# RWKV-7 recurrence of a hybrid decoder layer: work units of one head pair and 512 tokens, against blocks of two head pairs and 256 tokens

## The chip, the cores and the metric

The kernel runs on 1 core of one Trainium2 chip, in one launch. The metric is device time of one execution in microseconds (us). The core has TensorE (PE in the profile, with its weight loads shown as PEld), VectorE (DVE), ScalarE (ACT), GpSimd (POOL), and SyncE (SP, which here only issues DMAs). Every engine runs its own instruction stream in order and waits on semaphores where an operand comes from another.

## The reference, cut to what matters

One layer: RMSNorm, one input projection (1024 to 512 + 1792 columns), a pooling mixer on 512 columns, RWKV-7 time mixing with 8 heads of 64 on the rest, an output projection, then a squared-ReLU MLP (1024 to 4096 to 1024). A prompt of 1024 tokens and 8 single decode tokens go through it.

```python
def step(S, inp):
    r_t, w_t, k_t, v_t, aa_t, bb_t = inp          # aa = -kk, bb = kk * a
    sa = jnp.einsum('bhvk,bhk->bhv', S, aa_t)
    S = S * w_t[:, :, None, :] + sa[..., None] * bb_t[:, :, None, :] + v_t[..., None] * k_t[:, :, None, :]
    return S, jnp.einsum('bhvk,bhk->bhv', S, r_t)
S_final, y = lax.scan(step, S0, xs)               # over the tokens
y = ((y - mu) * lax.rsqrt(var + GN_EPS)).reshape(B, T, RWKV_W) * ln_x_g + ln_x_b
y = (y + bonus.reshape(B, T, RWKV_W)) * g
mix = jnp.concatenate([pool_out, rwkv_out], axis=-1) @ w_out
x = x + mix;  x = x + jnp.square(jax.nn.relu(rmsnorm(x) @ w_up)) @ w_down
```

## The kernel before

The scan over 1024 tokens is done in chunks of 64. Two heads of 64 fill the 128 partitions and are called a head pair; there are four, `hp` 0 to 3. A **unit** is one head pair and one half (512 tokens, 8 chunks); there are eight, numbered 0 to 7, four of half 0 first. For each unit run, in this order:

- `rkv` (R in the order string): r, k and v are projected (`gemm`, L175) and token-shifted.
- `stage1` (S): decays and keys; then for each of the two 256-token parts of the unit the operands of the recurrence. `AR` holds scaled kk and r with masked score planes, `RB` and `AA` further score planes, all made out of the score matmuls (`sc`, L402) by DVE (L407, L409) and ACT. `BK` has three planes, and its transposition `BKT` is made once for each head, out of a 128x128 transposition of which half is kept (L419, L420). `vt` are the transposed values, which ACT writes into `SV` (L427). `AR` and `RB` come from a ring of four static segments.
- `inverse` (I): `AA` of all 8 chunks and both heads goes through DRAM (`blk`, L466) into `Dg` (L469); DVE solves the small blocks in `Xs` (L484 to L501), ACT writes them to `Es`, DMAs put them through DRAM into `TX` (L510 to L514), and PE and ACT build the 64x64 inverses `TT` (L522 to L549). There is one buffer each of `Xs`, `Es`, `Dg`, `tm`, `TX`, so inverses go one after the other; `TT` and the DRAM buffers are double.
- `chain` (C): 8 steps, one a chunk, each depending on the one before. On PE: `pq` (L575), `pa` with the inverse (L579), `pu` (L582), and two `py` matmuls (L576, L583) that only make the output. On ACT: `sg` (state times decay), `Q` (copy of pq), two copies of pa into `SV` (L592). On DVE: two updates that write the new state (L591). PE waits for ACT's Q, ACT for pa, PE for SV, DVE for pu, and PE for the new state. fp32 matmuls show as two passes each in the trace (x2).
- `post`: after each 256 tokens the group norm, bonus and gate of the `y` rows; the result `ys` goes to DRAM as `mix` (L596), on POOL's queue, which also issues all weight loads (`wr`, L157).

A scheduler fixes each engine's order ahead of time from priorities (chain first, `LEAD`; then inverse, `LEADI`) and from the string ORDER, in which P are parts of the pooling mixer, T and L the second half's tokens and low-rank gates, D the 8 decode tokens with their own states `dS`. Work of low priority, mostly the projections, stands between the steps on PE. When the last chain and the decode tokens are through, SP loads the `mix` rows of the second half (`mr`, L851) and `x` (L837), the output projection (`mx`) is finished, and the MLP (`up`, `dn`) follows.

Of the kernel before, what the change touches and what calls it, by code (L numbers as in the profile page):

```python
# [15 lines left out]
P = 128  # L16
# [23 lines left out]
ORDER = """R0 S0 R1 I0 S1 Q C0 R2 S2 I1 C1 R3 S3 I2 P00 P01 T I3 P02 L R4 C2 S4 C3 R5 S5 I4 R6 C4 S6 I5 R7 C5 S7 I6 C6 P10 I7 P11 P12 D"""  # L40
NBV = 3
# [43 lines left out]
def _build(ctx, nc, tc, I, O, dbg):  # L85
# [108 lines left out]
    def token_block(b):  # L194
# [6 lines left out]
        acc = big(f"acc{b}", "f" if b % 2 else "g")[:, :512].rearrange("p (k t) -> p k t", k=2)  # L201
# [133 lines left out]
    Sf = [zp.tile([P, 64], F32, name=f"Sf{hp}") for hp in range(4)]  # L335

    def stage1(U):
        hp, nm = U.hp, U.nm
        zw, za, _ = Zt[U.half]
        U.gam = rcp.tile([P, 8], F32, tag="gam", name=f"gam{nm}", bufs=4)  # L340
        U.AA = rcp.tile([P, 8 * 64 + 16], F32, tag="AA", name=f"AA{nm}", bufs=2)
        GP.memset(U.AA[:, 512:], 0.0)
        A3 = U.AA[:, 0:512].rearrange("p (c t) -> p c t", t=64)
# [40 lines left out]
        act(U.gam, Ep[:, :, 64])  # L384
        for i in range(2):
# [3 lines left out]
            seg = ring[0]  # L389
            ring[0] = (seg + 1) % NSEG  # L390
            AR, RB = U.AR[i], U.RB[i] = ARs[seg], RBs[seg]
            for h in range(2):
                rr = R[h]
                V.tensor_tensor(AR[rr, :, 0, h, :], r3(kk[rr, ls]), Ep[rr, cc, 0:64], op=ALU.mult)
                V.tensor_tensor(AR[rr, :, 1, h, :], r3(U.r[rr, ls]), Ep[rr, cc, 1:65], op=ALU.mult)
                V.tensor_tensor(BK[rr, :, 2 * h, :], r3(t[rr, ls]), Em[rr, cc, 1:65], op=ALU.mult)
            V.tensor_tensor(BK[:, :, 1, :], r3(U.k[:, ls]), Em[:, cc, 1:65], op=ALU.mult)

            scs = [ps_m.tile([P, 4, 128], F32, tag="m", name=f"sc{nm}_{h}") for h in range(2)]
            for c in range(4):  # L400
                for h in range(2):
                    PE.matmul(scs[h][:, c, :], BK[R[h], c, h:h + 2, :], AR[R[h], c, :, h, :], start=True, stop=True)  # L402
            for h in range(2):
                rr, ro = R[h], R[1 - h]
                psc = scs[h]
                act(A3[rr, 4 * i:4 * i + 4, :], psc[rr, :, 0:64])
                V.tensor_tensor(RB[rr, :, h, :], psc[rr, :, 64:128],  # L407
                                MS[rr, 64:128].unsqueeze(1).to_broadcast([64, 4, 64]), op=ALU.mult)
                V.tensor_tensor(AR[ro, :, :, h, :], psc[ro].rearrange("p c (a t) -> p c a t", t=64),  # L409
                                MS[ro].rearrange("p (a t) -> p a t", t=64).unsqueeze(1).to_broadcast([64, 4, 2, 64]),  # L410
                                op=ALU.mult)

# [8 lines left out]
            pv = ps_m.tile([P, 2, 128], F32, tag="m", name=f"vt{nm}")  # L421
            for c in range(2):
                PE.transpose(pv[:, c, :], U.v[:, 256 * i + 128 * c:256 * i + 128 * c + 128], ident)
            S2 = SV.rearrange("p (c e) h t -> p c e h t", e=2)
            for h in range(2):
                for e in range(2):
                    act(S2[R[1 - h], :, e, h, :], pv[R[e], :, 64 * h:64 * h + 64])  # L427

# [4 lines left out]
    BK = rcp.tile([P, 4, 3, 64], F32, name="BK")  # L433
    ring = [0]
    for t in (*ARs, *RBs, BK):
        GP.memset(t, 0.0)
# [20 lines left out]
    def inverse(U):  # L457
# [13 lines left out]
        with tc.high_priority(offset=LEADI):  # L471
# [598 lines left out]
```

## Time and profile before

| | |
|---|---|
| median of 3 runs | 1367.27 us (1367.04 to 1373.31) |
| the profiled execution | 1363.59 us, span 1361.8 us, mean granted clock 0.992 |
| busy over the span | PE 1298.1 us (95%), PEld 1144.8 (84%), DVE 823.2 (60%), ACT 592.4 (43%), POOL 156.3 (11%) |
| 0 to 577 us: projections, pooling mixer, recurrence, decode tokens | PE 525.14, DVE 435.38, ACT 424.71 |
| 577 us to the end: output projection of the second half, MLP | PE almost without a gap |

The page names the 20 costliest groups of instructions first; nearly all of them are of `gemm`. The recurrence is spread over some 300 small groups and is read from the timeline and from the tiles' answers instead. Matmul ends are modelled, so PE's busy time also contains time in which it was not at its peak.

### The profile page before, as it was taken

Reading aid. Unit: us, or ns where it says so; the run is one execution under the profiler, and the core shown is the slowest. Engines: PE = TensorE matmul, PEld = TensorE weight load, DVE = VectorE, ACT = ScalarE, POOL = GpSimd, SP = SyncE. Lnnn points to the kernel's source line nnn. Section 1 sums busy time; section 2 is a strip of 40 time slices with the busy share of each in tenths; the row PEclk is TensorE's granted clock in tenths of the full one; section 3 lists DMA queues with packets and bytes.
Section 4 is the critical chain, followed back from the end, with each engine's and each line's share of the span. In section 5 each row is a group of like instructions: output and inputs, shape, how many; then the busy total and the mean of one; then the engine's idle time right before and its main releaser. Section 6 shows DMA issues by size and latency. Waiting matters only on the chain.

```text
span 1361.8 us, 24570 instructions
## 1 busy us (share of the span) xinstructions
PE 1298.1 (95%) x9844; PEld 1144.8 (84%) x9844; DVE 823.2 (60%) x1816; ACT 592.4 (43%) x1466; POOL 156.3 (11%) x306
## 2 busy tenths in 40 slices
PE   5999998999999889999999999999999999999996
PEld 5987777888777777798999999999999999999986
DVE  8887687768778666749634435445344354453447
ACT  7668777866777767526211112112111121121122
POOL 3201001210101021120100000000000000000000
PEclk9999999999999999999999999999999999999998
DMA  6322223321322362531111111111111111111103
GB/s 196 106 58 58 70 47 94 109 70 42 79 55 51 75 198 95 197 101 47 53 49 47 47 47 47 47 47 47 48 46 49 48 46 48 45 48 50 47 5 125
DMA packets 75315, 94.82 MB, mean 70 GB/s; under 512 B 46168, under 2 KB 52440, under 8 KB 75192
## 3 DMA queue, kind: packets, MB, share of 16 engines
q0 software_dynamic: 20480, 66.04, 15.0%
q1 hardware_dynamic: 53392, 25.36, 7.2%
q10 hardware_dynamic: 1328, 1.85, 0.4%
q8 instruction: 77, 1.26, 0.4%
q14 instruction: 38, 0.31, 0.1%
HBM read 79.67 MB, written 13.78 MB: 69 GB/s over the span
## 4 chain that ended last, share of the span: by engine, by line
PE 75%; DVE 10%; ACT 9%; issue 2%; DMA 2%; POOL 1%; DVEq 0%; SPq 0%; POOLq 0%; ACTq 0%
PE dn L175 26%; PE up L175 26%; PE pj L175 7%; PE mx L175 5%; ACT SV L92 2%; PE pcs L582 1%; DVE tm L498 1%; PE pcs L579 1%; ACT Es L92 1%; ACT TT L92 1%; PE bkt L419 1%; PE pcs L575 1%; PE sc L402 1%; DVE wl L165 1%; PE py L583 1%
## 5 line engine op out<-in xcount | busy, mean ns | idle before, releaser
L92 ACT ACTIVATE wh<-wr 128x512 fp32r<-128x512 f32 x230 | 143.6, 626 | 353.2 <-PE dn L175 276.2
L175 PE MATMUL up<-h2h,wl 128*128 128x260 f32 (+1 forms) x768 | 245.5, 320 | 0.0
L175 PE MATMUL up<-h2h,wh 128*128 128x260 f32 (+1 forms) x768 | 245.0, 320 | 0.5 <-DVE u L912 0.5
L175 PE MATMUL up<-h2l,wh 128*128 128x260 f32 (+1 forms) x768 | 244.8, 319 | 0.0
L175 PE MATMUL dn<-uh,wl 128*128 128x512 f32 (+1 forms) x720 | 231.0, 321 | 0.0
L175 PE MATMUL dn<-ul,wh 128*128 128x512 f32 (+1 forms) x720 | 230.6, 320 | 0.0
L175 PE MATMUL dn<-uh,wh 128*128 128x512 f32 (+1 forms) x720 | 230.3, 320 | 0.0
L951 DVE TENSOR_TENSOR x<-dn,x 128x260 f32<-128x260 f32 (+1 forms) x192 | 99.0, 516 | 189.9 <-PE dn L175 189.9
L175 PE MATMUL pj<-xh,wh 128*128 128x256 f32 (+1 forms) x576 | 173.5, 301 | 14.3 <-ACT wh L92 13.9
L165 DVE TENSOR_TENSOR wl<-wr,wh 128x512 fp32r<-128x512 f32 x230 | 156.3, 684 | 45.1 <-ACT wh L92 38.2
L175 PE MATMUL pj<-xl,wh 128*128 128x256 f32 (+1 forms) x576 | 171.6, 298 | 0.0
L175 PE MATMUL pj<-xh,wl 128*128 128x256 f32 (+1 forms) x576 | 168.9, 293 | 0.0
L175 PEld LDWEIGHTS up<-h2l,wh 128*128 128x128 f32 x768 | 144.5, 188 | 12.2 <-DVE h2l L894 0.4
L175 PEld LDWEIGHTS up<-h2h,wh 128*128 128x128 f32 x768 | 144.1, 188 | 11.7 <-DVE u L912 0.9
L175 PEld LDWEIGHTS up<-h2h,wl 128*128 128x128 f32 x768 | 144.4, 188 | 11.1
L92 ACT ACTIVATE uh<-u 128x260 fp32r<-128x260 f32 (+1 forms) x96 | 47.2, 492 | 238.5 <-DVE u L913 238.5
L175 PEld LDWEIGHTS dn<-ul,wh 128*128 128x128 f32 x720 | 135.4, 188 | 10.9 <-issue 0.2
L175 PEld LDWEIGHTS dn<-uh,wh 128*128 128x128 f32 x720 | 135.7, 188 | 10.5
L175 PEld LDWEIGHTS dn<-uh,wl 128*128 128x128 f32 x720 | 135.4, 188 | 10.6 <-issue 0.2
L175 PEld LDWEIGHTS pj<-xh,wh 128*128 128x128 f32 x576 | 110.5, 192 | 18.8 <-ACT wh L92 14.2
L912 DVE SCALAR_TENSOR_TENSOR u<-up,rs 128x260 f32<-128x260 f32 (+1 forms) x96 | 49.5, 516 | 120.7 <-PE up L175 114.2
L175 PEld LDWEIGHTS pj<-xl,wh 128*128 128x128 f32 x576 | 110.5, 192 | 3.1 <-issue 1.9
(295 smaller groups left out, 2184.2 us busy)
## 6 DMA issues: line engine op xcount, KB each, us to landing
wr<-in_w_in POOLq DMA_DIRECT2D x72, 256.0 KB, 2.9
wr<-in_w_up POOLq DMA_DIRECT2D x64, 256.0 KB, 2.9
wr<-in_w_down POOLq DMA_DIRECT2D x64, 256.0 KB, 2.9
wr<-in_w_out POOLq DMA_DIRECT2D x26, 256.0 KB, 3.1
xr<-in_xT SPq DMA_DIRECT2D x16, 256.0 KB, 3.7
mr<-mix SPq DMA_DIRECT2D x8, 260.0 KB, 3.2
x<-in_xT SPq DMA_DIRECT2D x2, 1040.0 KB, 8.3
blk<-AA SPq DMA_DIRECT2D x16, 128.0 KB, 2.7
```

Source lines behind the costliest of these rows:

```text
L92: A.activation(out, in_, func, bias=bias, scale=scale, **k)
L165: V.tensor_tensor(l[:, :w], raw[:, :w], f32(h[:, :w]), op=ALU.subtract)
L175: PE.matmul(ps, lhs, rhs, start=i == 0, stop=i == n - 1)
L402: PE.matmul(scs[h][:, c, :], BK[R[h], c, h:h + 2, :], AR[R[h], c, :, h, :], start=True, stop=True)
L419: PE.transpose(pt[:, c, :], BK[:, c, h:h + 2, :].rearrange("p a t -> p (a t)"), ident)
L498: V.tensor_tensor(pr[:, q], l[:, q].unsqueeze(2).to_broadcast([64, m, m, m]), r[:, q].rearrange("p k j -> p j k").unsqueeze(1).to_broadcas ...
L575: PE.matmul(pq, AR[:, c, 0, :, :], SV[:, c, :, :], start=True, stop=True)
L579: PE.matmul(pa, TT[:, g, :, :], Q, start=True, stop=True)
L582: PE.matmul(pu, BKT[:, c, :, :], SV[:, c, :, :], start=True, stop=True)
L583: PE.matmul(py[:, c, :, :], SV[:, c, :, :], RB[:, c, :, :], start=False, stop=True)
L912: V.scalar_tensor_tensor(u, ps[:, :n], 0.0, rs2[:, cs], ALU.max, ALU.mult)
L951: V.tensor_tensor(d, ps[:, :n], d, op=ALU.add)
```

## The change

A **block** is now two head pairs (`q` 0: pairs 0 and 1, `q` 1: pairs 2 and 3) and 256 tokens (`b` 0 to 3): eight blocks of 4 chunks instead of eight units of 8. `R` and `S` stay with units; `I` and `C` go over blocks.

- A chain is 4 steps, and each step does both pairs: two matmuls of a kind where there was one, one `Q` copy of 128x256, two `SV` copies of 64x2x64, two `sg`, four DVE updates. `post` is merged into the chain and works on 512 columns of both pairs; both `py` buffers (`ps_y`) belong to one block.
- An inverse takes 4 chunks of two units, so it needs the scores of both.
- `BK` has two planes with the head's own plane at its place, so one transposition a chunk yields both heads: 64 `bkt` transpositions instead of 128, 16 ACT copies of 128x512 instead of 32 of 128x256. `RB` is written by one operation on 128 partitions, and `AR`'s second plane is no longer masked (AR<-sc is 64x256 instead of 64x512).
- `SV` is twice as large with 2 buffers; `BKT` is static, four segments; the segments are given out by `seg` so that a block's two units hold the ones that the next pair's unit needs.
- ORDER is written anew, NBV is 4 instead of 3, the accumulator `acc` takes another tag.

```diff
-ORDER = """R0 S0 R1 I0 S1 Q C0 R2 S2 I1 C1 R3 S3 I2 P00 P01 T I3 P02 L R4 C2 S4 C3 R5 S5 I4 R6 C4 S6 I5 R7 C5 S7 I6 C6 P10 I7 P11 P12 D"""
-NBV = 3
+ORDER = """R0 S0 R1 S1 P00 I0 Q P01 C0 I1 P02 C1 R2 S2 R3 T S3 L I2 R4 C2 I3 R5 C3 S4 S5 I4 R6 C4 I5 R7 C5 S6 S7 I6 P10 C6 I7 P11 P12 D"""
+NBV = 4
...
+            u, pair = hp % 2, hp // 2 + 2 * U.half
+            B = blocks[2 * pair + i]
...
+            seg = u + 2 * i if pair % 2 else 2 * u + i
+            AR, RB, BKT = B.AR[u], B.RB[u], B.BKT[u] = ARs[seg], RBs[seg], BKTs[seg]
...
-                    PE.matmul(scs[h][:, c, :], BK[R[h], c, h:h + 2, :], AR[R[h], c, :, h, :], start=True, stop=True)
+                    PE.matmul(scs[h][:, c, :], BK[R[h], c, :, :], AR[R[h], c, :, h, :], start=True, stop=True)
...
-                for c in range(4):
-                    PE.transpose(pt[:, c, :], BK[:, c, h:h + 2, :].rearrange("p a t -> p (a t)"), ident)
-                act(BKT[:, :, h, :], pt[:, :, rr])
...
+            for c in range(4):
+                PE.transpose(pt[:, c, :], BK[:, c, :, :].rearrange("p a t -> p (a t)"), ident)
+            act(BKT.rearrange("p c h t -> p c (h t)"), pt)
...
+        for c in range(4):
...
+            for u in range(2):
+                PE.matmul(pq[:, u], B.AR[u][:, c, 0, :, :], SV[:, c, u], start=True, stop=True)
+                PE.matmul(py[u][:, c, :, :], SV[:, c, u], B.AR[u][:, c, 1, :, :], start=True, stop=False)
...
+            act(Q, pq)
+            for u in range(2):
+                PE.matmul(pa[:, u], TT[:, 4 * u + c, :, :], Q[:, u], start=True, stop=True)
+            for u in range(2):
+                act(sg[:, u], SV[:, c, u], scale=gam[u])
             for h in range(2):
...
+                act(SV[R[h], c, :, h, :], pa[R[h], :, h, :])
+            for u in range(2):
+                PE.matmul(pu[:, u], B.BKT[u][:, c, :, :], SV[:, c, u], start=True, stop=True)
...
+            for h in range(2):
+                for u in range(2):
+                    dst = Sq[R[h], u, :] if c == 3 else SV[R[h], c + 1, u, h, :]
+                    V.scalar_tensor_tensor(dst, pu[R[h], u, h, :], gam[u][R[h]], sg[R[h], u, h, :], ALU.mult, ALU.add)
```

PE, within one step of the first chain, where projections (`pj`) fill the row between the steps. Before:

```order
L175 MATMUL pj11_1_2124<-xh1_206,wh_2090 128x256
L175 MATMUL pj11_1_2124<-xl1_207,wh_2090 128x256
L582 MATMUL pcs_108<-SV0_0_742,BKT0_0_741 128x128
L583 MATMUL py0_0_1312<-RB0_142,SV0_0_742 128x128
L175 MATMUL pj11_1_2124<-xh1_206,wl_2091 128x256
L175 MATMUL pj11_1_2124<-xh1_206,wh_2090 128x256
L175 MATMUL pj11_1_2124<-xl1_207,wh_2090 128x256
L175 MATMUL pj11_1_2124<-xh1_206,wl_2091 128x256
L175 MATMUL pj11_1_2124<-xh1_206,wh_2090 128x256
L575 MATMUL pcs_108<-SV0_0_742,AR0_138 128x128
L576 MATMUL py0_0_1312<-AR0_138,SV0_0_742 128x128
```

After, from `pa` of a joint step (pairs 0 and 1 of the first half) to its last `py`:

```order
L592 MATMUL pcs_108<-Q0_0_2_1647,TT0_159 128x128 x2
L183 MATMUL pj14_1_2164<-xl1_208,wh_2124 128x256
L183 MATMUL pj14_1_2164<-xh1_207,wl_2125 128x256
L183 MATMUL pj14_1_2164<-xh1_207,wh_2124 128x256
L183 MATMUL pj14_1_2164<-xl1_208,wh_2124 128x256
L183 MATMUL pj14_1_2164<-xh1_207,wl_2125 128x256
L598 MATMUL pcs_108<-SV0_0_1103,BKT0_144 128x128
L598 MATMUL pcs_108<-SV0_0_1103,BKT2_146 128x128
L600 MATMUL py0_0_0_1598<-RB0_140,SV0_0_1103 128x128
L600 MATMUL py0_0_1_1599<-RB2_142,SV0_0_1103 128x128
L183 MATMUL pj14_1_2164<-xh1_207,wh_2124 128x256
```

Each kind of matmul now comes twice in a row, once for each pair (`AR0` and `AR2` are the segments of units 0 and 1).

PE, where the scores of the last unit's first 256 tokens (`sc3_2`) stand. Before, they come behind the first step of unit 6's chain (`SV2_2`), whose inverse is of its own:

```order
L603 MATMUL py1_3_5401<-ys1_3_5454,cst_86 128x256
L575 MATMUL pcs_108<-SV2_2_4893,AR0_138 128x128
L175 MATMUL pj0_3_5967<-xh3_2942,wh_5895 128x264
L402 MATMUL sc3_2_0_5519<-AR2_140,BK_146 128x128
L606 MATMUL py1_3_5401<-q1_3_5458,cst_86 128x256
L402 MATMUL sc3_2_1_5520<-AR2_140,BK_146 128x128
L402 MATMUL sc3_2_0_5519<-AR2_140,BK_146 128x128
L402 MATMUL sc3_2_1_5520<-AR2_140,BK_146 128x128
```

After, they come behind the last `pq` of block 5's chain (`SV0_3`: pairs 0 and 1, tokens 768 to 1023), with which they share the segment `AR1`:

```order
L587 MATMUL pcs_108<-SV0_3_4091,AR1_137 128x128
L587 MATMUL pcs_108<-SV0_3_4091,AR3_139 128x128
L588 MATMUL py0_3_1_4962<-AR3_139,SV0_3_4091 128x128
L383 MATMUL pb3_1_5210<-bv3_1_5208,cst_86 128x512
L592 MATMUL pcs_108<-Q0_3_3_5031,TT1_160 128x128 x2
L414 MATMUL sc3_2_0_5224<-AR1_137,BK_148 128x128 x3
L598 MATMUL pcs_108<-SV0_3_4091,BKT1_145 128x128
L598 MATMUL pcs_108<-SV0_3_4091,BKT3_147 128x128
```

The last unit's scores moved from beside the chains of its own half to the end of the chain of the pair before; the inverses of blocks 6 and 7 both need them.

DVE, at the start of the last inverse (`Xs` from `Dg`). Before, unit 7's inverse (`Dg3_1`) begins among the state updates of unit 6's chain (`SV2_3`):

```order
L645 TENSOR_TENSOR dq_6369<-dk_6370 128x32
L753 SCALAR_TENSOR_TENSOR d1_1_5926<-d1_1_5926,u1_1_5925 128x512
L748 SCALAR_TENSOR_TENSOR d1_1_5926<-poold_164,u1_1_5925 128x8
L165 TENSOR_TENSOR wl_6637<-wr_6634,wh_6636 128x512
L591 SCALAR_TENSOR_TENSOR SV2_3_4937<-pcs_108,gam2_1_4826,sg2_1_3_5789 64x64 x2
L484 COPY Xs_156<-Dg3_1_6034 64x8
L492 TENSOR_TENSOR tm3_1_6035<-Dg3_1_6034,Xs_156 64x16
```

After, block 7's inverse (`Dg1_3`) begins shortly after the last DVE operation (`XB1_2`) of block 6's, and block 6's chain has not begun:

```order
L551 STREAM_TRANSPOSE XB1_2_5401<-TX1_2_5328 128x256
L150 TENSOR_SCALAR da_6036<-da_6036 128x32
L657 TENSOR_TENSOR dw_6039<-pwd_6054,vec_87 128x32
L173 TENSOR_TENSOR wl_6580<-wr_6577,wh_6579 128x512
L150 TENSOR_SCALAR dw_6039<-dw_6039 128x32
L665 TENSOR_TENSOR dvec_132<-dk_6038,dq_6037 128x4x8
L666 TENSOR_TENSOR dvec_132<-dvec_132,da_6036 128x4x8
L683 TENSOR_TENSOR dW0_6307<-dS0_6045,dvec_132 128x512
L501 COPY Xs_157<-Dg1_3_5702 64x8
L509 TENSOR_TENSOR tm1_3_5703<-Dg1_3_5702,Xs_157 64x16
```

The two inverses of a pair of blocks now stand directly one behind the other, ahead of both chains.

## Rows read from the trace of the kernel before

**Rows 1.** The page's first part: busy time, share of the span, instructions.

```profile
PE 1298.1 (95%) x9844; PEld 1144.8 (84%) x9844; DVE 823.2 (60%) x1816; ACT 592.4 (43%) x1466; POOL 156.3 (11%) x306
```

**Rows 2.** Busy time of each engine in stretches: from:to, length, busy of PE, PEld, DVE, ACT, POOL with numbers of instructions, granted clock, DMA share, GB/s.

```profile
82.00:112.00 30.00, 26.84 (x381) 24.13 (x379) 24.86 (x65) 19.39 (x50) 2.80 (x6) 1.00 0.22 61
...
460.30:491.00 30.70, 26.45 (x341) 21.98 (x339) 20.45 (x51) 21.71 (x59) 6.50 (x12) 1.00 0.43 127
...
0.00:577.00 577.00, 525.14 (x4877) 443.86 (x4877) 435.38 (x1075) 424.71 (x1157) 83.33 (x171) 0.99 0.32 93
577.00:612.00 35.00, 35.00 (x293) 35.00 (x293) 14.71 (x30) 8.42 (x14) 7.44 (x13) 1.00 0.36 117
```

**Rows 3.** Timeline of one chain step of unit 0 (start, duration, engine, line, operation; x2 are the two passes of one fp32 matmul, or two instructions).

```profile
122.80 0.49 PE L575 MATMUL pcs<-SV,AR 128*128 128x128 f32 x2
...
123.37 0.26 ACT L92 ACTIVATE Q<-pcs 128x128 f32<-128x128 f32 x1
...
123.94 0.38 PE L579 MATMUL pcs<-Q,TT 128*128 128x128 f32 x2
124.36 0.45 ACT L92 ACTIVATE SV<-pcs 64x64 f32<-64x64 f32 x2 [0.21 <-PE pcs L579]
...
124.86 0.49 PE L582 MATMUL pcs<-SV,BKT 128*128 128x128 f32 x2
...
125.54 0.58 DVE L591 SCALAR_TENSOR_TENSOR SV<-pcs,gam,sg 64x64 f32<-64x64 f32 x2
...
126.17 0.49 PE L575 MATMUL pcs<-SV,AR 128*128 128x128 f32 x2
```

**Rows 4.** Timeline, PE alone: `pq` of the last steps of the chains of units 3, 5 and 7, and ahead of them of the first step of unit 3.

```profile
251.29 0.40 PE L575 MATMUL pcs<-SV,AR 128*128 128x128 f32 x2
...
276.65 0.49 PE L575 MATMUL pcs<-SV,AR 128*128 128x128 f32 x2
...
429.66 0.49 PE L575 MATMUL pcs<-SV,AR 128*128 128x128 f32 x2
...
522.38 0.38 PE L575 MATMUL pcs<-SV,AR 128*128 128x128 f32 x2
```

**Rows 5.** Timeline: where inverses begin (`blk`), where DVE takes them up (`Xs<-Dg`) and where `TT` is written last; units 0, 1, 3, 5 and 7.

```profile
72.42 1.36 SPq L466 DMA_DIRECT2D blk<-AA  x2
...
81.97 0.15 DVE L484 COPY Xs<-Dg 64x8 f32<-64x8 f32 x1
...
110.88 2.15 SPq L466 DMA_DIRECT2D blk<-AA  x2
...
111.93 0.76 ACT L92 ACTIVATE TT<-pi 32x256 f32<-32x256 f32 x2
...
200.28 2.01 SPq L466 DMA_DIRECT2D blk<-AA  x2
...
358.49 1.27 SPq L466 DMA_DIRECT2D blk<-AA  x2
...
450.12 1.28 SPq L466 DMA_DIRECT2D blk<-AA  x2
...
460.30 0.17 DVE L484 COPY Xs<-Dg 64x8 f32<-64x8 f32 x1
...
490.18 0.76 ACT L92 ACTIVATE TT<-pi 32x256 f32<-32x256 f32 x2
```

**Rows 6.** Groups of instructions up to 577 us, each shape apart: busy time, mean ns of one, idle time before and its releasers.

```profile
L419 PE MATMUL bkt<-cst,BK 128*128 128x128 f32 x128 | 21.3, 280 | 2.6 <-DVE AR L409 2.5
...
L92 ACT ACTIVATE SV<-pcs 64x64 f32<-64x64 f32 x128 | 27.6, 216 | 14.5 <-PE pcs L579 12.7
L92 ACT ACTIVATE sg<-SV,gam 128x128 f32<-128x128 f32 x64 | 24.8, 395 | 11.9 <-DVE SV L591 11.6
...
...
L92 ACT ACTIVATE BKT<-bkt 128x256 f32<-128x256 f32 x32 | 12.1, 381 | 16.5 <-PE bkt L419 16.2
...
L409 DVE TENSOR_TENSOR AR<-sc,cst 64x512 f32<-64x512 f32 x32 | 22.0, 688 | 0.4
```

**Rows 7.** Timeline: four of the transpositions `bkt` in a row.

```profile
114.32 0.60 PE L419 MATMUL bkt<-cst,BK 128*128 128x128 f32 x4
```

**Rows 8.** The answer on the tile `pcs`, in which pq, pa and pu lie: idle time of an engine just before its instruction on the tile, by what ended it (us, times), all engines together.

```profile
  PE pcs L582: 29.8, 34
  ACT Q L92: 17.1, 33
  ACT SV L92: 13.6, 46
```

**Rows 9.** Timeline behind the last chain: the group norm's first matmul, the last operation of `post`, what SP issues, and the chain that ended last (two of its pieces: start, length, what).

```profile
525.78 0.70 PE L603 MATMUL py<-ys,cst 128*128 128x256 f32 x2
...
531.42 0.48 DVE L613 SCALAR_TENSOR_TENSOR ys<-ys,vec,py 128x256 f32<-128x256 f32 x1 [1.50 <-PE py L612]
...
554.95 1.75 SPq L700 DMA_DIRECT2D mix<-da  x4
556.75 12.78 SPq L851 DMA_DIRECT2D mr<-mix  x8
...
569.58 6.91 DMA x<-in_xT
...
576.99 3.02 PE mx L175 x23
```

More of the change, by code (lines that the diff above doesn't have):

```diff
@@ L333, in rkv @@
             shifted(base + U.hp, U.half, t)
-    Sf = [zp.tile([P, 64], F32, name=f"Sf{hp}") for hp in range(4)]
+    Sf = [zp.tile([P, 2, 64], F32, name=f"Sf{q}") for q in range(2)]
+    blocks = [Block(n) for n in range(8)]
     def stage1(U):
@@ L421, in stage1 @@
[L421 to L427 removed]
+                act(A3[rr], psc[rr, :, 0:64])
+                V.tensor_tensor(RB[:, :, h, :], psc[:, :, 64:128], MS[:, 64:128].unsqueeze(1).to_broadcast([P, 4, 64]),
+                                op=ALU.mult)
@@ new lines, in stage1 @@
+                V.tensor_tensor(AR[ro, :, 0, h, :], psc[ro, :, 0:64], MS[ro, 0:64].unsqueeze(1).to_broadcast([64, 4, 64]),
+                                op=ALU.mult)
+            pt = ps_m.tile([P, 4, 128], F32, tag="m", name=f"bkt{nm}")
+            for c in range(4):
+                PE.transpose(pt[:, c, :], BK[:, c, :, :].rearrange("p a t -> p (a t)"), ident)
+            act(BKT.rearrange("p c h t -> p c (h t)"), pt)
+        if u:
+            for i in range(2):
+                token_rows(blocks[2 * pair + i])
@@ new lines, in token_rows @@
+    def token_rows(B):
+        i = B.b % 2
+        B.SV = rcp.tile([P, 4, 2, 2, 64], F32, tag="SV", name=f"SV{B.nm}", bufs=2)
+        S2 = B.SV.rearrange("p (c e) u h t -> p c e u h t", e=2)
+        pv = ps_m.tile([P, 2, 2, 128], F32, tag="m", name=f"vt{B.nm}")
+        for u in range(2):
+            for c in range(2):
+                PE.transpose(pv[:, c, u, :], B.U[u].v[:, 256 * i + 128 * c:256 * i + 128 * c + 128], ident)
+        for h in range(2):
+            for e in range(2):
+                act(S2[R[1 - h], :, e, :, h, :], pv[R[e], :, :, 64 * h:64 * h + 64])
@@ L431, in _build @@
     ARs = [rcp.tile([P, 4, 2, 2, 64], F32, name=f"AR{i}") for i in range(NSEG)]
     RBs = [rcp.tile([P, 4, 2, 64], F32, name=f"RB{i}") for i in range(NSEG)]
[L433 to L436, printed above, removed]
+    BKTs = [rcp.tile([P, 4, 2, 64], F32, name=f"BKT{i}") for i in range(NSEG)]
+    BK = rcp.tile([P, 4, 2, 64], F32, name="BK")
+    for t in ARs:
+        for h in range(2):
+            GP.memset(t[R[1 - h], :, 1, h, :], 0.0)
@@ L600, in post @@
-    def post(hp, nm, ps, ys, n, bv, zg, out):
-        pm, pv = ps[:, 256:512], ps[:, 0:256]
-        PE.matmul(pm[:, :n], CJ, ys, start=True, stop=True)
-        q = rcp.tile([P, 256], F32, tag="q", name=f"q{nm}", bufs=1)
-        act(q[:, :n], pm[:, :n], AF.Square)
-        PE.matmul(pv[:, :n], BO, q[:, :n], start=True, stop=True)
-        act(q[:, :n], pv[:, :n], AF.Ln, bias=EPSG, scale=1.0 / 64)
-        act(q[:, :n], q[:, :n], AF.Exp, scale=-0.5)
-        V.tensor_tensor(out, pm[:, :n], q[:, :n], op=ALU.mult)
-        V.scalar_tensor_tensor(out, out, col(V_LG, hp), bv, ALU.mult, ALU.add)
-        pg = pm
-        PE.matmul(pg[:, :n], glu[:, hp * P:(hp + 1) * P], zg, start=True, stop=True)
-        V.scalar_tensor_tensor(out, out, col(V_LB, hp), pg[:, :n], ALU.add, ALU.mult)
+        B.TT = TT
@@ L815, in decode_start @@
         next(dec[0])
-    calls = {"R": rkv, "S": stage1, "I": inverse, "C": lead_chain}
+    calls = {"R": (rkv, units), "S": (stage1, units), "I": (inverse, blocks), "C": (lead_chain, blocks)}
     for c in ORDER.split():
         if c[0] in calls:
-            calls[c[0]](units[int(c[1])])
+            call, of = calls[c[0]]
+            call(of[int(c[1])])
         elif c[0] == "P":
@@ L862, in out_block @@
         V.tensor_tensor(d, ps[:, :q], d, op=ALU.add)
-    lead_chain(units[7])
+    lead_chain(blocks[7])
     open_x1(0)
```

153 lines of the change are left out of this document (72 added, 81 removed).

## The prediction

> **What bounds the kernel now.** I read the stretches first. From 0 to 577 us PE is busy for 525 us, DVE for 435 and ACT for 425; behind that PE has 35 of 35 us [rows 1, 2]. The change touches only the part before 577 us, which ends when `mx` of the second half begins at 576.99 [rows 9]; the MLP behind it is the same code with PE full, so whatever the change does to that point it does to the time. The profiled execution took 1363.59 us (span 1361.8); the median of the runs is 3.7 us above it. I work out a shift of the point 577 us and put it on the median.
>
> PE at 91% (525 of 577) looks like the bound, but its busy time counts matmuls that trickle out one at a time, so I next read one chain step. From `pq` to the next `pq` the trace shows 122.80, Q at 123.37, pa at 123.94, SV at 124.36, pu at 124.86, update at 125.54, `pq` at 126.17: 3.37 us in which each link waits for the one before [rows 3]. Unit 3's chain makes seven steps in 25.4 us, 3.62 each [rows 4]. That latency, eight times per unit, is one thing in the way. The other is the inverse: from `blk` at 72.42 to DVE's start at 81.97 is 9.6 us, and on to the end of `TT` at 112.69 another 30.7; for unit 7 it is 450.12, 460.30, 490.94, so 40.8 in all, of which 30.6 behind DVE's start [rows 5]. In those two stretches no engine but PE is above 25 of 30 us, and PE's 26 to 27 are mostly other work [rows 2]: an inverse is a latency too. The third reading is the end: the last `pq` is at 522.38, `post` is through at 531.9, but the decode tokens (`mix<-da`) only at 554.95, then eight `mr` loads are issued in 12.8 us, then `x` takes 6.9 [rows 4, 9]. So the last chain has some 23 us of room before the decode tokens' work, which is woven into the same streams.
>
> **The change part by part.** *Chain steps.* A joint step has everything twice on the engines, but one latency. On top of 3.37 us: a second pq, pa and pu add about 0.22 to 0.27 each, as one matmul of two passes lasts 0.38 to 0.49 [rows 3]; the copies into SV go from 0.45 to about 0.55, Q from 0.26 to the 0.38 that a 128x256 copy takes [rows 3, 6]; two more updates on DVE add up to 0.58 [rows 3]; the two `sg` of 0.395 [rows 6] now stand between Q and the SV copies on ACT, where pa's time covers most of them. Sum 3.37 + 0.7 + 0.1 + 0.1 + 0.58 = 4.9, and with 3.62 as the base 5.1. Between the ends 4.6 (updates overlapped) and 5.8 (sg uncovered) I take 5.1, since unit 3's steps are the longest undisturbed run. 64 steps of 3.62 (232 us) become 32 of 5.1 (163): 69 us of chain latency go. Only what lies on the path counts, though.
>
> *Inverses.* There are still eight of equal size, with one `Xs`, `Es` and `Dg`. Before, a unit's inverse ran beside the chain of the unit ahead of it, and its scores were ready early. Now both inverses of a pair of blocks need the scores of the pair's second unit, and they come one straight behind the other on DVE, ahead of both chains. The second `TT` comes 30.7 us behind the first if DVE takes the second up at once [rows 5]; DVE's other operations stand between, so I take 33. Likewise I take 42 from `blk` to `TT` for the 40.3 and 40.8 of units 0 and 7. While the chain of the first block (20 us) is hidden under that second inverse, the chain of the second block, 4 x 5.1, is not.
>
> *Fewer operations.* 64 transpositions go: four in a row take 0.60 [rows 7], so 64 x 0.15 = 9.6 us of PE, 18 at the 280 ns that a lone one lasts [rows 6]. On ACT 16 copies of `BKT` less and wider ones, 32 wide Q instead of 64 narrow, 64 SV copies of 271 ns for 128 of 216: about 25 us in all [rows 6]. On DVE AR<-sc is half as wide, 32 x some 0.27 = 9 us less [rows 6], but BK is written in four half operations instead of three, which takes that back in part. ACT and DVE are at 74% and 75%, so these are worth nothing by themselves beyond quicker answers to PE. The wider `post` and the double `SV` cost no more work than before; both `py` buffers now belong to one block, so block n+1 cannot begin before block n's `post` (6 us before, 525.78 to 531.9 [rows 9], some 9 with twice the columns), and that lies under the second inverse.
>
> *The path.* I walk the pairs. Scores of unit 1 were ready at 110.88, held back by priority [rows 5]; in the new order they come ahead of the first inverse, and with S0 R1 S1 and part of P00 before it I put DVE's start at 100 instead of 82. First `TT` at 100 + 32 = 132, second at 165, end of block 1's chain at 185; unit 1's chain before ended near there too. Unit 3's scores stand on PE behind R2, S2, R3, T; before, its `blk` left at 200 [rows 5], and with about the same PE work ahead I take 205 to 222. `TT` 42 later, 247 to 264; second +33; chain +20: end of block 3 at 300 to 318, against 280 before. Unit 5's scores were at hand before 358 [rows 5]; the first block needs only their first part, 350 to 358, so `TT` at 392 to 400, second 425 to 433, last `pq` of block 5 at 441 to 449 (429.66 before [rows 4]). Unit 7's scores share segments with block 5 and come 5 us behind that last step, so `blk` of block 6 at 446 to 454, as unit 7's was at 450 [rows 5]. `TT` 42 later at 488 to 496, second 521 to 529, last `pq` 15 later at 536 to 544 and the end of the chain at 540 to 549. That is 14 to 22 us later than 522 [rows 4], on a chain that had 23 us of room. `post` at 549 to 558; its store and `mr` load are some 6 us; 555 to 564. Meanwhile the decode tokens end near 553 as before (same steps, spread over the same stretch), six `mr` loads follow, then `x` (now ahead of the last two), which takes 6.9 [rows 9]: 553 + 2 + 9.6 + 6.9 = 571.5, with `mh` and `x` update 573 to 576. Sum: 575, 2 us earlier than 577. On the median that is **1365 us**, no change that a measurement of this kernel can tell (about 0.5%, 7 us).
>
> **The rivals.** *Faster: PE's waits in the chain go.* The idle time before instructions on `pcs` is 29.8 us for pu (DVE waiting), 17.1 for Q and 13.6 for SV [rows 8]; PE waits for the last two, 31 us. With half as many steps and twice the matmuls in each, half of these go (15), and the 9.6 of transpositions are truly off PE: up to 25, if the projections that fill the chains then end earlier and the scores of unit 7 with them. For it: PE is the busiest engine; against it: at each pair the scores are followed by 42 + 33 + 20 us of latency into which the order must put PE work, and the last pair has hardly any left. I take 13 of the 25: 1354. It decides if block 5's chain ends before 440.
>
> *PE alone counts.* If only PE's work mattered, 9.6 us less gives 1357.7. The Trainium skill (Perfetto Trace Analysis, Identifying the Most-Contended Engine) says that the most-contended engine is the one to optimize, and that for TensorE weight-load busy time, not matmul busy time, is the measure. By that measure PEld has 444 of 577 us, close to DVE's 435 [rows 2], so the rows do not make PE the sole bound here.
>
> *Slower: the two inverses in a row at the end.* If block 5's last step is at 455 or later (steps of 5.8, or the second inverse slowed to 40 by DVE's other work), the last chain ends at 555 to 562, `post` at 571, and `mr` 6 and 7 are the last loads: `mx` at 585 to 595. It also holds the decode tokens, whose state loads stand behind block 7's inverse on SP. That is +8 to +18, taken at +13: 1380. For it: DVE is busy 25 of 30 us in the first inverse [rows 2]; it decides from an end of the last chain at 553.
>
> **How the numbers follow.** No change (1360 to 1374) 0.40; faster 0.32, of which 0.08 is PE's work alone and the rest the waits, with a floor of 25 less, 1342; slower 0.28, up to +25, 1392, if the half of each pair is lost as in block 3's 20 to 38 us. Leaving a tenth off each end, the range is 1345 to 1388.
>
> **What would show it.** After: `pq` to `pq` in a joint step near 5.1 us (right between 4.6 and 5.8); second `TT` of a pair 31 to 33 us behind the first; `blk` of block 6 at 446 to 454; last `pq` at 536 to 544; decode's end near 553; `mx` of the second half at 573 to 578. If the two inverses overlap, or unit 7's scores come before 440, the forecast is too high; if the last chain ends past 553, it is too low. A PE whose stretch to 577 is no shorter by the 9.6 us would speak against the PE rival.

## The result, and the profile after

Four runs of the changed kernel took 1377.28 us in the median (1376.39 to 1379.30), four of the kernel before beside them 1368.01: ratio 1.0062, 95% interval 1.0033 to 1.0090. It is slower by 9.3 us; forecast was 1365, no change. The profiled execution's span is 1377.5 us against 1361.8.

Busy time of the whole span (the page's first part), then in stretches, first of the changed kernel, then of the kernel before:

```profile
PE 1304.7 (95%) x9748; PEld 1149.1 (83%) x9748; DVE 809.3 (59%) x1824; ACT 567.7 (41%) x1310; POOL 152.1 (11%) x301
```

```profile
0.00:577.00 577.00, 524.16 (x4747) 441.24 (x4748) 412.89 (x1069) 393.21 (x990) 77.99 (x164) 0.96 0.31 89
204.00:238.00 34.00, 21.73 (x118) 18.05 (x117) 25.64 (x69) 20.57 (x49) 4.11 (x8) 0.70 0.28 73
459.00:476.00 17.00, 13.63 (x45) 9.84 (x46) 11.22 (x29) 12.60 (x34) 2.15 (x4) 0.70 0.73 204
476.00:493.00 17.00, 17.00 (x243) 13.08 (x242) 7.32 (x15) 10.55 (x29) 2.71 (x5) 0.80 0.36 101
493.00:510.00 17.00, 16.01 (x98) 12.56 (x97) 14.48 (x48) 10.64 (x40) 1.08 (x2) 0.90 0.46 170
```

```profile
459.00:476.00 17.00, 15.69 (x108) 13.50 (x107) 11.17 (x33) 11.76 (x35) 1.71 (x4) 1.00 0.24 56
476.00:493.00 17.00, 14.05 (x256) 11.34 (x255) 9.85 (x20) 13.17 (x34) 6.41 (x12) 1.00 0.64 205
493.00:510.00 17.00, 15.63 (x76) 12.52 (x75) 11.38 (x32) 9.48 (x33) 1.09 (x2) 0.90 0.59 200
```

Over the whole span ACT lost 25 us and DVE 14 [rows 1], as the fewer operations promise; up to 577 us the difference is larger, 32 and 22 [rows 2], because the changed kernel has not come as far by then. PE lost nothing: 524 us again up to 577, but at a granted clock of 0.96 instead of 0.99. The lower of the clock's two levels (1.2 GHz) is half of the upper (2.4 GHz), so 0.03 of the mean stands for some 35 us more of the 577 at the lower level. The clock is low in and behind two holes in which PE waits, one at the half boundary (204 to 238 us), one ahead of the last pair (459 us).

A joint chain step, block 7's, on the timeline (x4: two matmuls of two passes):

```profile
540.38 0.61 PE L587 MATMUL pcs<-SV,AR 128*128 128x128 f32 x4
...
541.03 0.39 ACT L100 ACTIVATE Q<-pcs 128x256 f32<-128x256 f32 x1
541.52 0.66 PE L592 MATMUL pcs<-Q,TT 128*128 128x128 f32 x4
542.27 0.56 ACT L100 ACTIVATE SV<-pcs 64x128 f32<-64x128 f32 x2 [0.86 <-PE pcs L592]
542.88 0.71 PE L598 MATMUL pcs<-SV,BKT 128*128 128x128 f32 x4
...
545.78 0.61 PE L587 MATMUL pcs<-SV,AR 128*128 128x128 f32 x4
...
550.85 0.61 PE L587 MATMUL pcs<-SV,AR 128*128 128x128 f32 x4
```

From `pq` to `pq` 5.4 and 5.1 us. Two single steps took 7.2 [rows 4]: the step's latency gain is there. Now the last pair's inverses, timeline: `blk` of block 6, DVE's start, `Es` and `TT` of block 6, then the same of block 7:

```profile
448.47 2.86 SPq L483 DMA_DIRECT2D blk<-AA  x2
...
457.34 0.17 DVE L501 COPY Xs<-Dg 64x8 f32<-64x8 f32 x1
...
466.76 2.36 ACT L100 ACTIVATE Es<-Xs 32x256 f32<-32x256 f32 x4
...
490.21 0.76 ACT L100 ACTIVATE TT<-pi 32x256 f32<-32x256 f32 x2 [0.92 <-PE pi L561]
...
494.35 0.16 DVE L501 COPY Xs<-Dg 64x8 f32<-64x8 f32 x1
...
511.60 2.41 ACT L100 ACTIVATE Es<-Xs 32x256 f32<-32x256 f32 x4
...
534.18 0.75 ACT L100 ACTIVATE TT<-pi 32x256 f32<-32x256 f32 x2
```

Block 6 needs 42.5 us from `blk` to `TT`. Block 7's `TT` comes 44.0 behind it; its part on DVE, from `Xs<-Dg` to `Es`, begins 3.4 us behind block 6's `TT` and lasts 17.3 us where block 6's took 9.4; from `Es` to `TT` 23.3 us pass (24.2 in block 6). What DVE's stream holds in that part:

```profile
494.62 0.16 DVE L509 TENSOR_TENSOR tm<-Dg,Xs 64x16 f32<-64x16 f32 x1
495.97 0.69 DVE L173 TENSOR_TENSOR wl<-wr,wh 128x512 fp32r<-128x512 f32 x1 [1.20 <-ACT wh L100]
497.11 0.98 DVE L604 SCALAR_TENSOR_TENSOR SV<-pcs,gam,sg 64x64 f32<-64x64 f32 x4 [0.45 <-PE pcs L598]
498.12 0.17 DVE L511 TENSOR_TENSOR tw<-tm 64x16 f32<-64x16 f32 x1
498.21 0.18 DVE L668 TENSOR_TENSOR da<-da,ona 128x32 f32<-128x32 f32 x1
```

Between two of the inverse's small operations (`tm`, then `tw`, 3.3 us) stand a weight split (`wl`) that waits for ACT and the state updates of block 6's chain that wait for PE; behind `tw` come operations of the decode tokens. The last `pq` is at 550.85, where it was 522.38 [rows 4]. The end, SP's timeline and two pieces of the chain that ended last:

```profile
559.93 1.76 SPq L716 DMA_DIRECT2D mix<-da  x4
563.32 10.17 SPq L868 DMA_DIRECT2D mr<-mix  x6
575.89 0.94 SPq L854 DMA_DIRECT2D x<-in_xT  x2
576.99 1.14 SPq L868 DMA_DIRECT2D mr<-mix  x2
```

```profile
577.64 10.08 DMA mr<-mix
...
590.11 34.98 PE mx L183 x270
```

The decode tokens end (`mix<-da`) 5.0 us later than before, `x` is issued 6.3 later, a last `mr` load takes 10.1 us beside it, and the full stream of `mx` begins at 590.11 instead of 576.99 [rows 9]: 13.1 of the 15.7 us of span. The rest came behind it; the span from 592 to 600 us ran at a granted clock of 0.78. What SP waited for there (waits of SP, 550 to 584 us: in total, times, longest):

```profile
SPq L868 <- DVE ml L870: 4.6, 1, 4.6
...
SPq L854 <- PE mx L183: 2.5, 1, 2.5
SPq L868 <- DVE ys L625: 1.6, 1, 1.6
```

The first `mr` waits for block 7's `post` (`ys`), a later one for the split of an earlier row (`ml`), which on DVE stands behind results of the first half's `mx`, and `x` for that `mx` on PE. In the kernel before, SP waits there neither for `ys` nor for `mx`. By these waits the late chain reaches the loads mostly by way of the streams of PE and DVE, in which the first half's `mx` stands among and behind it.

### The profile page after: what moved, and what is told of

It reads as the page before. It is cut to its first block, busy times and chain, and to the rows that moved or that the text cites. A ratio compares the mean times of both kernels' runs of the same rounds, so it can differ in the third digit from the quotient of the medians.

```text
span 1377.5 us, 24283 instructions
## 1 busy us (share of the span) xinstructions
PE 1304.7 (95%) x9748; PEld 1149.1 (83%) x9748; DVE 809.3 (59%) x1824; ACT 567.7 (41%) x1310; POOL 152.1 (11%) x301
## 4 chain that ended last, share of the span: by engine, by line
PE 78%; ACT 9%; DVE 7%; issue 3%; DMA 3%; POOL 0%; SPq 0%; DVEq 0%; ACTq 0%; POOLq 0%
PE dn L183 26%; PE up L183 26%; PE pj L183 7%; PE mx L183 6%; PE sc L414 2%; ACT SV L100 1%; PE pcs L598 1%; PE pcs L592 1%; ACT Es L100 1%; DMA mr<-mix 1%; PE py L588 1%; ACT ys L100 1%; DVE wl L173 1%; DMA wr<-in_w_in 1%; DVE tm L515 1%
```

## The experiments

Theory: the last chain, which waits for two inverses one behind the other, used up its room and holds up the last loads. Rivals: PE's work and its order set the end; low clock behind holes does; the order of the last loads does. Three kernels leave out part of the computation, as their expectations say. Times are medians, ratios to the kernel before on the same chip; kernels measured on different chips are compared by their ratios, the changed kernel's being 1.0062 (1.0033 to 1.0090).

| run | us | ratio, 95% interval |
|---|---|---|
| b_onetr | 1365.07 | 0.9983 (0.9964 to 1.0001) |
| a_leadi | 1377.93 | 1.0079 (1.0052 to 1.0106) |
| a_noi7 | 1364.99 | 0.9987 (0.9971 to 1.0004) |
| a_xlast | 1375.79 | 1.0067 (1.0046 to 1.0088) |
| a_split | 1379.37 | 1.0080 (1.0051 to 1.0109) |
| a_nbv3 | 1390.59 | 1.0158 (1.0110 to 1.0206) |
| b_noi7 | 1362.62 | 0.9961 (0.9939 to 0.9982) |
| a_pools | 1387.59 | 1.0138 (1.0106 to 1.0170) |
| a_own | 1376.65 | 1.0061 (1.0037 to 1.0085) |
| b_own | 1362.58 | 0.9961 (0.9945 to 0.9977) |
| a_warm | 1370.65 | 1.0020 (1.0000 to 1.0041) |
| a_ownwarm | 1381.23 | 1.0099 (1.0073 to 1.0126) |
| a_warmb | 1380.86 | 1.0103 (1.0075 to 1.0130) |
| a_warmt | 1373.44 | 1.0049 (1.0026 to 1.0072) |
| a_noi7warm | 1363.88 | 0.9981 (0.9961 to 1.0001) |
| b_ownwarm | 1368.90 | 1.0025 (1.0005 to 1.0044) |
| a_xdep | 1377.14 | 1.0071 (1.0049 to 1.0094) |

**The last inverse left out.** In the changed kernel and, as control, in the kernel before:

```diff
+            if c == "I7":
+                blocks[7].TT = blocks[6].TT
+                continue
             call(of[int(c[1])])
```

> The changed kernel without the last inverse: block 7 uses the inverses of block 6, so its results are not those of the reference. Theory (the last chain waits for two inverses one behind the other, and the last loads wait for it): block 7's chain runs right behind block 6's, the last pq at 525 to 530, the loads of the second half start near 556 again, and the time falls by 10 to 16: 1361 to 1367. Rival (PE's work sets the end): only the inverse's matmuls go, about 3 us: 1373 to 1375.

> The kernel before without the last inverse: unit 7 uses the inverses of unit 6, so its results are not those of the reference. Theory (before, the last chain had 23 us of room behind it, because the decode tokens ended at 555): only the inverse's own work goes, 0 to 4 us less, 1363 to 1367. If the last chain set the end of the kernel before too (rival), the loss of the changed kernel was no use of room, and the time falls as in the changed kernel by about 12: 1355.

a_noi7's last `pq`, SP's end, and where full `mx`, its stream without gaps, begins (timeline of PE, of SP, the chain that ended last):

```profile
535.90 0.61 PE L587 MATMUL pcs<-SV,AR 128*128 128x128 f32 x4
```

```profile
553.64 1.75 SPq L716 DMA_DIRECT2D mix<-da  x4
555.44 12.73 SPq L871 DMA_DIRECT2D mr<-mix  x8
568.21 0.98 SPq L857 DMA_DIRECT2D x<-in_xT  x2
```

```profile
576.63 36.94 PE mx L183 x294
```

The last chain comes 15 us earlier (expected 21 to 26), and the whole loss is gone: 12.3 us by the medians, 0.75% or 10 by the ratios. Everything from `mix<-da` on is back at the times of [rows 9], though the clock is not:

```profile
0.00:577.00 577.00, 523.00 (x4590) 441.33 (x4591) 416.34 (x1066) 392.36 (x984) 79.06 (x166) 0.96 0.31 93
```

That is the clock of the changed kernel, without its loss. The same cut in the kernel before, last `pq` and full `mx` again:

```profile
497.43 0.38 PE L575 MATMUL pcs<-SV,AR 128*128 128x128 f32 x2
```

```profile
576.89 35.41 PE mx L175 x294
```

Its last `pq` comes 25 us earlier, and full `mx` begins where it did (576.99 in [rows 9]): before, the last chain had room. Its time fell by 0.39%, some 5 us and a little over the expected 4; the trace does not show where, and the interval of this ratio is too wide to tell it from the 0.75% with certainty. The traces make the difference: 15 us of the last chain bring full `mx` 13.5 us forward in the changed kernel, 25 us bring nothing in the kernel before. That speaks against the rival that PE's work alone sets the end, as the matmuls of one inverse are some 3 us of PE. One thing is mixed in: a_noi7 also issues all eight `mr` ahead of `x`, where the changed kernel has `x` ahead of the last two.

**One part of the change alone, and the fastest version.** b_onetr puts the single transposition, RB and AR into the kernel before; b_own adds the buffers of a_own below.

```diff
-                V.tensor_tensor(BK[rr, :, 2 * h, :], r3(t[rr, ls]), Em[rr, cc, 1:65], op=ALU.mult)
-            V.tensor_tensor(BK[:, :, 1, :], r3(U.k[:, ls]), Em[:, cc, 1:65], op=ALU.mult)
+                V.tensor_tensor(BK[rr, :, h, :], r3(t[rr, ls]), Em[rr, cc, 1:65], op=ALU.mult)
+                V.tensor_tensor(BK[rr, :, 1 - h, :], r3(U.k[rr, ls]), Em[rr, cc, 1:65], op=ALU.mult)
...
-            for h in range(2):
...
+            pt = ps_m.tile([P, 4, 128], F32, tag="m", name=f"bkt{nm}")
```

> The kernel before, with one part of the change alone: one transposition a chunk for both heads, RB written at 128 partitions at once, AR masked in one plane. If PE's work sets the time up to 577 us, 64 transpositions of 0.15 us less give -9.6 us: 1358. If the latencies of inverse and chain set it, as I hold, the freed time is waited away: 1365 to 1368, within 3 us of before.

> The kernel before with one transposition (b_onetr) and the same buffers for XB and Z2. Before, each unit's inverse begins when its scores are there, and the end has room behind the last chain: 1362 to 1367, within 3 us of b_onetr (1365.1), by the theory. If a buffer shared by two inverses cost time by itself in any order (rival), the gain is as in the changed kernel, some 10: 1355.

b_onetr's stretch up to 577 us:

```profile
0.00:577.00 577.00, 537.01 (x4815) 457.66 (x4816) 431.74 (x1092) 423.77 (x1141) 82.90 (x171) 0.96 0.32 94
```

64 transpositions less, and PE is busy 12 us longer than before [rows 2], at 0.96 instead of 0.99. The time falls by 0.17%, an interval that touches no change and leaves out the 9.6 us (0.7%). The time came out as expected; that the freed work was waited away is not shown, since the lower clock can have used it up as well. b_own is 0.39% faster than the kernel before; that its buffers add to b_onetr is not separated by the intervals.

**Ways to shorten the second inverse.** a_leadi puts the inverse ahead of the chain; a_split gives XB and Z2 tiles of their own, for which NBV must be 3 (control: a_nbv3); a_own puts both in Z's buffer, leaves NBV at 4 and gives `sg` one buffer.

```diff
-LEADI = 500
-LEADJ = 500
+LEADI = 700
+LEADJ = 700
```

```diff
-            XB = rcp.tile([P, 8, 32], F32, tag="Dg", name=f"XB{B.nm}")
+            XB = rcp.tile([P, 8, 32], F32, tag="Z", name=f"XB{B.nm}")
...
-            Z2 = rcp.tile([P, 8, 32], F32, tag="tm", name=f"Z2{B.nm}")
+            Z2 = rcp.tile([P, 8, 32], F32, tag="Z", name=f"Z2{B.nm}")
```

> The changed kernel, the inverse given priority over the chain (LEADI and LEADJ 700 instead of 500). In the changed kernel the last inverse took 17 us on DVE from Xs<-Dg to Es, against 10 for the others, with updates of block 6's chain and decode operations between its steps. If this late second inverse sets the end (theory), it takes about 33 instead of 44 us behind the first, the last pq comes at 541 to 545 instead of 550.9, and the time falls by 5 to 10: 1367 to 1372. If PE's work sets the end (rival; mx of the first half ends at 570.5 in both kernels), no change within 3 us.

> The changed kernel with a buffer of its own for XB and for Z2 (both shared one with the next inverse's Dg and tm) and NBV 3 to make room. DVE's part of the second inverse of a pair then may begin when the first has written Es, not when its XB and Z2 are used up. Theory (two inverses one behind the other set the end): the second TT comes 15 to 25 us behind the first instead of 33 to 44, the last pq at 525 to 537, time 1360 to 1368. Rival (PE's work and its order set the end): within 3 us of the changed kernel, 1374 to 1380.

> The changed kernel with NBV 3 alone, the control for a_split. Both theories: unit 3's or unit 7's bonus values wait a little longer, within 3 us of the changed kernel, 1375 to 1380.

> The changed kernel with NBV 4 as it is, and XB and Z2 in the buffer of Z (instead of the next inverse's Dg and tm); sg has one buffer to make room. It is a_split without the loss that NBV 3 brought (a_nbv3 took 1390.6, a_split 1379.4). Theory (two inverses one behind the other set the end through the last chain): the second TT of the last pair 20 to 30 us behind the first, last pq at 535 to 542, 1364 to 1371. Rival (the decode tokens and mx of the first half set the end by PE's order, whatever the last inverse does): 1374 to 1380.

a_leadi, block 7 (timeline):

```profile
499.42 0.16 DVE L501 COPY Xs<-Dg 64x8 f32<-64x8 f32 x1
...
510.94 2.41 ACT L100 ACTIVATE Es<-Xs 32x256 f32<-32x256 f32 x4
...
534.77 0.74 ACT L100 ACTIVATE TT<-pi 32x256 f32<-32x256 f32 x2
```

DVE's part fell from 17.3 to 11.5 us and the second `TT` stood 40.4 us behind the first instead of 44.0 (expected 33), but the first came 4 us later and the second when it had come before: my explanation by DVE's stream is a part of the 44 us and not the one that decides. a_nbv3 fell outside its expectation (13 us slower for one bonus buffer less). Against it a_split gains 11, but not against the changed kernel; at NBV 4 a_own gains nothing:

```profile
501.59 0.76 ACT L100 ACTIVATE TT<-pi 32x256 f32<-32x256 f32 x2
...
530.30 0.37 ACT L100 ACTIVATE TT<-pi 32x256 f32<-32x256 f32 x1
```

```profile
566.04 1.75 SPq L716 DMA_DIRECT2D mix<-da  x4
567.84 12.63 SPq L868 DMA_DIRECT2D mr<-mix  x8
```

```profile
510.00:544.00 34.00, 32.55 (x370) 23.88 (x370) 16.33 (x39) 27.25 (x90) 2.16 (x4) 1.00 0.19 63
544.00:578.00 34.00, 33.68 (x171) 26.11 (x171) 22.97 (x46) 20.09 (x44) 6.46 (x12) 1.00 0.34 108
```

The second `TT` is 28 us behind the first instead of 44, but the first is 11 later, the second 4 earlier, and the decode tokens end at 566 instead of 560, with PE almost full from 510 on. What the inverse gained was lost on the other path to the loads, that of the decode tokens. In all three (a_leadi, a_split, a_own) the rival's number came true and mine did not: none of them brought the last chain far enough forward (last `pq` at 550.4, 545.4 and 547.4).

**Order of work and loads.** a_pools moves P00 and P01 behind R3 and P02 behind S3; a_xlast issues `x` behind the `mr` loads in the program; a_xdep makes its load wait for the last row.

```diff
+            if half:
+                V.tensor_copy(x1[1][:, k, 0:1], f32(last[0][0])[:, 0:1])
             SY.dma_start(x1[half][:, k:k + 4, :], I["xT"][:, k:k + 4, c0:c0 + n])
```

> The changed kernel with the first half's pooling work (P00, P01, P02 in the order string) put behind R3, S3 instead of beside the first inverses and chains. From 204 to 238 us PE was busy for 21.7 of 34 us at a granted clock of 0.70, waiting for unit 3's scores. If such holes at the half boundary cost time that comes out at the end (rival to the theory of the last pair), pools fill it, pair 2 begins 5 to 8 us earlier and the time falls by as much: 1369 to 1372. If the last pair's latency is what counts, the end moves only as far as block 5's chain does: 0 to 4 us less, 1373 to 1377.

> The changed kernel, x of the second half loaded behind the last mix rows instead of between rows 5 and 6. In the changed kernel the last mr load took 10.1 us beside x, and mx went on at 590.1. If the order of these loads costs (theory), mr lands some 6 us earlier and mx starts on it while x is under way; mx then waits for x only at its first addition: 3 to 5 us less, 1372 to 1374. If only the late start counts (rival; the same bytes have to come), no change within 2 us, or up to 2 slower.

> The changed kernel with x of the second half made to wait for the last mix row: one column of x is first written from that row's values, which the load then overwrites. If the order of the last loads costs what the other runs suggest (x ahead: the last mr takes 10 to 13 us instead of 3.5, mx full 14 to 17 us behind the issue of x instead of 7 to 8), the full stream of mx begins at 584 to 586 instead of 590.1 and the time falls by 5 to 8: 1369 to 1372. If only the last chain's lateness counts and the bytes take their time in any order, within 2 us: 1375 to 1379.

Moving the pools made it slower by 10; neither number held. a_xlast gained nothing by its ratio, with one of the two `x` loads still ahead of the last rows. In a_xdep the last `mr` takes 3.0 us and `x` 6.0, but `x` is issued only at 582.27, behind the wait that I added, and full `mx` begins at 588.77 (expected 584 to 586):

```profile
576.48 3.04 DMA mr<-mix
...
582.27 6.00 DMA x<-in_xT
...
588.77 37.07 PE mx L183 x294
```

So the 10.1 us of that load come with the loads of `x` issued just ahead of it; whether it shares the way with them or waits behind them is not shown. What the order is worth in time stays open, as the forced wait ate what it brought.

**PE kept at work in its holes.** 14 matmuls that nothing uses, 8 at the boundary (a_warmb alone), 6 ahead of the last pair (a_warmt alone):

```diff
+        if U is units[7]:
+            warm(CJ[R[1], :], blocks[7].SV[R[1], :, :, 0, :], 6)
```

> The changed kernel with 14 matmuls more that nothing uses (128x512 fp32, into the inverse's PSUM tile): 3 and 5 where PE waited for unit 3's values between 195 and 215 us, 6 behind block 7's values, where PE waited from 461 to 468. In the changed kernel the granted clock was 0.70 from 204 to 238 and 0.70, 0.80 and 0.90 in the three 17 us behind 459, and mx matmuls of 128x512 there followed each other at 0.43 us instead of 0.23. If this low clock behind holes costs (rival to the last pair alone), keeping PE at work lifts the clock in these stretches to 0.9 or more and the time falls by 4 to 10 although PE does more: 1367 to 1373. If not, the time is the same or up to 8 higher: 1376 to 1385.

> The same 14 matmuls in a_own (XB and Z2 in the buffer of Z), which alone left the time as it was (1376.7), its last TT 4 us earlier but the clock 0.78 to 0.82 from 459 to 510. If late second inverse and low clock both hold up the end, so that taking away one shows the other, both together give 1362 to 1370, more than either alone. If the clock doesn't count, 1376 to 1384.

> a_warm with its first 8 matmuls alone, in the hole at the half boundary (195 to 215 us). If the low clock there costs time that comes out at the end, most of a_warm's 6.6 us: 1371 to 1373. If later waits swallow it, the changed kernel's 1377, within 2 us; this is what I expect, since pair 2's start moves little and the second half has waits of its own: 1374 to 1378.

> a_warm with its last 6 matmuls alone, in the hole ahead of the last pair (461 to 468 us). If the low clock of 0.70 to 0.90 behind that hole (459 to 510) is what delays the last chain and mx of the first half, 4 to 7 us less than the changed kernel: 1370 to 1373. If the boundary's hole was it, 1376 to 1380.

> The changed kernel without the last inverse (block 7 uses block 6's, so its results are not those of the reference) and with the 14 matmuls of a_warm. a_noi7 took 1365.0. If low clock and late last chain are two causes, both go: 1357 to 1361. If the 14 matmuls helped only by bringing the last chain forward, no better than a_noi7: 1363 to 1368.

> b_own (1362.6) with two unused matmuls ahead of each of the eight poolings' first matmul, where PE waited for pool weights or DVE (226 to 248, 480 to 490 us; granted clock 0.70 to 0.84 in the first, 0.66 to 0.76 from 493 to 510). If low clock behind holes costs here too, 3 to 6 less: 1357 to 1360. If b_own's end is held by decode and loads, 1361 to 1366.

a_warm, stretches:

```profile
459.00:476.00 17.00, 14.56 (x50) 8.73 (x49) 7.83 (x13) 13.31 (x34) 2.69 (x5) 0.96 0.74 221
476.00:493.00 17.00, 15.92 (x243) 12.63 (x243) 9.54 (x24) 9.49 (x26) 2.70 (x5) 0.84 0.26 75
```

The clock rises to 0.96 in the hole and the ratio falls from 1.0062 to 1.0020, some 6 us, although PE does more (the two intervals just overlap). Of its parts the six at the last pair bring 0.13%, within the intervals, and the eight at the boundary make it 0.4% slower, so the two do not add up to the gain. Three things keep low clock from being a cause of its own. a_noi7 has the changed kernel's clock of 0.96 and no loss. a_noi7warm is no faster than a_noi7 (0.9981 and 0.9987), so the gain goes with the last chain, whose last `pq` a_warm has at 544.4. And a_warm and a_warmt also issue all eight `mr` ahead of `x`, so the order of loads is mixed in. What the lower clock adds to the lateness of the last chain is not separated. b_ownwarm lifts the clock from 493 to 510 us of b_own from 0.70 to 1.00 and is 0.64% slower; a_ownwarm is 0.38% slower than a_own. a_warmb (1380.86) and b_ownwarm (1368.90) lie outside both of their expectations.

**The last chain and the end, over all traces.** With the last `pq` at 497.4 (b_noi7), 522.4 (before) and 535.9 (a_noi7), full `mx` begins at 576.9, 577.0 and 576.6. With the last `pq` at 544.4 (a_warm), 550.9 (the changed kernel), 559.1 (a_pools) and 561.9 (a_nbv3), it begins at 582.9, 590.1, 598.7 and 599.8; the other versions of the changed kernel with a last `pq` from 545 to 552 lie within some 4 us of the line through these. So the last chain costs nothing up to a point between 536 and 544 us and about its own delay behind it. Clock and order of loads vary among these kernels too. b_ownwarm does not fit in: its last `pq` is at 522.1 and full `mx` at 582.7, with its decode tokens ending at 560.4.

## Why the prediction was wrong

- *Chain step 5.1 us*: right (5.1 to 5.4).
- *Scores of the last unit, `blk` of block 6 at 446 to 454*: right (448.5). The walk held within some 9 us through three pairs (last `pq` of block 1 at 176, its chain's end forecast for 185; of block 5 at 442.5, forecast 441 to 449); first `TT` of the last pair at 491.0, within 488 to 496.
- *"second +33"*: **the step that failed.** I took one inverse's undisturbed 30.7 us and a little; at the last pair it was 44.0 (35.2, 33.7 and 38.2 at the three pairs before). Of the 11 us over the forecast, some 8 are in DVE's part (17.3 us, 9.4 in block 6) and 3.4 in its late start; the rest, from `Es` to `TT`, was no longer than block 6's. On DVE the second inverse stands among block 6's chain and the decode tokens. The last `pq` came at 550.9, not 536 to 544.
- *23 us of room*: **mis-sized.** a_noi7, 13.5 us later than before, lost nothing; a_warm, 22.0 later, already lost 5.9 at full `mx`. With the delay counted one to one behind the point where it begins, that is some 16 us of room (my estimate from a_warm), and the changed kernel's 28.5 less 16 is close to the 13.1 that it lost. So with the last `pq` at the late end of the forecast, 544, the end would have moved too.
- *Decode's end at 553, "573 to 576"*: mis-sized. It was 560, and `x` and the last rows, which I let run side by side in 6.9 us, took 12 from the issue of `x`. This term was no better founded than its sum: the row of 6.9 had `x` alone [rows 9].
- *The slower rival*: its number, 1380, was near, and its sign for the last chain (an end behind 553) came true, at 555. Its other condition did not: block 5's last `pq` came at 442.5, not 455. It was mainly the second inverse, at 44 instead of its 40.
- *The PE rival*: as a forecast, that 9.6 us less of PE's work show in the time, refuted by b_onetr. a_noi7, which gains 10 us for some 3 of PE's work, speaks against it too. PE's order is another matter, as SP's waits show. The Trainium skill (Perfetto Trace Analysis, Identifying the Most-Contended Engine) would optimize the most contended engine. Here PEld, the busiest by its measure, is at 441 of 577 us, ACT lost 25 us and DVE 14 over the span, and the time rose. What a_noi7 took away is mainly a latency, and no engine's sum.

What stays open: whether shortening block 7's inverse by itself would bring the time back, since every version that tried it moved other work (priority moved the wait, didn't remove it), and the worth of the order of the last loads.

## What to carry to other kernels

Joining two serial chains shortened the steps here (5.1 to 5.4 us for two that took 7.2), but ask what the joined unit must wait for: here two inverses through single buffers. Price the last unit by itself, in the neighbourhood in which it runs, since earlier ones have cover and it has little. And room is not the whole gap to the next piece of work: with a gap of 23 us, a last chain 22 us later already cost 6 (a_warm). Work taken off PE, ACT or DVE in such a stretch brought nothing that could be told from no change (b_onetr).

## What the runs showed of the hardware

In these runs the granted clock and the time did not move together. a_noi7 and the changed kernel both ran their first 577 us at 0.96, and took 1364.99 and 1377.28 us (ratios 0.9987 and 1.0062); filling holes lifted the clock in a_warm (0.70 to 0.96 in the hole), with a gain, and in b_ownwarm (0.70 to 1.00), with a loss. The Trainium skill (TensorE: Matmul & The Clock Gate, Why this matters for your kernels) advises against idle gaps of PE. The clock agrees (0.70 to 0.90 in and behind the holes of the changed kernel); of the six versions in which holes were filled, the time fell in one (a_warm), stayed within the intervals in two (a_warmt, a_noi7warm) and rose in three (a_warmb, a_ownwarm, b_ownwarm); only b_ownwarm's interval lies wholly apart from that of the version without. One `mr` row of 260 KB lands in 3.0 us without the two loads of `x` ahead of it (a_xdep) and in 10.1 with them.
